# Two transformer blocks on one core: attention heads prepared in slices, key halves copied by DMA, chunk heads split out of PSUM, late consumers of powers, 128-row gates, offset half-width weights

## The chip, the cores and the metric

The kernel runs on one core of a Trainium2 chip. The metric is the time of one execution on the device, in microseconds (us). A core has five engines with a queue of instructions each: TensorE (PE, matrix products; the load of the stationary operand is shown apart as PEld), VectorE (DVE), ScalarE (ACT), GpSimd (POOL) and SyncE (SP, which here only issues DMAs). Each engine works through its queue in order and waits on semaphores for what other engines or DMAs must have finished. Products are summed in PSUM, everything else lies in SBUF.

## The reference

512 tokens of width 1024 pass through two blocks, in f32.

```python
# block 1 (first_block)
proj = rmsnorm(h) @ w_in            # q, k, v: 8 heads of 64; u, g of the gated branch; 8 forget gates
c = cumsum(log_sigmoid(gates))      # per head, along the tokens
p = softmax(causal(q k^T / 8 + c[query] - c[key]));  att = p v
uv = gelu(u, g);  sg = u * (w_spatial (128x128, lower triangle) @ rmsnorm(g) + b_spatial)
h = h + concat(att, sg) @ w_out
h = h + (silu(g) * a) @ w_down      # a, g: halves of the causal 3-tap convolution of rmsnorm(h) @ w_up
x = rmsnorm(h, norm_final_g)
# block 2 (second_block), with modulation from silu(c) @ w_ada
proj = modulated(rmsnorm(x)) @ w_in # latents of q (256) and kv (128), a rope key (32), ca: 8 chunk heads of 64
mla:  q = rope(rmsnorm(rmsnorm(q_lat) @ w_q_up)); k, v from kv_lat; mask by chunks of 64 tokens
ca:   q, k = rmsnorm(ca_q) g_q, rmsnorm(ca_k) g_k; softmax(q k^T / 8 + rel_bias)
x = x + g_a * (concat(mla, ca) @ w_out);  x = x + g_m * conv_ffn(modulated(rmsnorm(x)))
```

## The kernel before

Every product is made from halves: an operand is split into a high part (rounded to the fp32r format of TensorE) and a low part (the rest), and three matmuls hi·hi, hi·lo, lo·hi are summed. The names end in h and l (xnh, xnl; whi, wlo).

Weights stream from DRAM. `make_plan` (L276) lists all pieces in order of use, at most 128x1024 each. For each piece `load_split` (L335) issues a load on SP's queue into `wraw` (3 buffers), ACT casts it to `whi`, and DVE (for a few pieces POOL) subtracts to get `wlo`. A piece is requested when the product two pieces ahead of it takes its own. A plan entry ends with an offset: some pieces are written 192 elements into their buffers (`SKEW`). Before, only token-major pieces carry it, in which the weights are the moving operand.

The program has five stages: mix of block 1 (0 to 241.6 us of the span), FFN of block 1 (to 588), start of block 2 (to 664), attention of block 2 (to 882.6), FFN of block 2.

Attention is cut in strips: one head times 128 queries; 32 strips in block 1, 64 in block 2 (32 of chunk heads, then 32 of latent heads). A strip is: scores on PE (`strip_scores`, s<-kh,qs and s<-kl,qs); DVE adds the bias and takes the row minimum of the negated scores (L590, s and st); ACT takes the exponential (L594, p); one strip later PE transposes p (L603, s<-ident,p), DVE or ACT copies it out of PSUM (L605, pt); one strip after that PE multiplies it with the values (o<-vv,pt or o<-vc,pt). After eight strips a pair of heads is divided by its sums (L687, att), transposed (L695) and split into `mix`.

Between the strips of `attention` (L612) two lists of jobs advance (class `Fill`): `fill` holds products for PE, which cover the chain from scores to p; `bg` holds norms for DVE, ACT and POOL. `fill.upto(name)` runs all fill work up to a named product at once. PE's order is the order in which the program is written. The other engines are ordered by a list scheduler; `high_priority(offset)` moves work forward (AHEAD, 40) or back (BEHIND, 60) in it. Once set, each engine keeps its order.

A head is prepared `ahead` strips before its first scores, 2 in block 1, 4 in block 2. In block 1 that is a PE product which spreads one row of cumulated gates over 128 rows (mm<-cum,pick, 64 rows of contraction), the copies ch and cm, and `stack` (L659). That stacks the high and the low half of q on 128 partitions (qs) and the key parts kh and kl twice, so that two matmuls do the work of three: ACT copies kh twice, DVE subtracts kl twice, 64x512 each (L668, L669). In block 2 a pair of chunk heads is transposed into PSUM (L1596), copied to qf and kf (L1599, L1601), and stacked from there.

Reciprocal square roots of the norms are powers on POOL (L523). Three products use them on DVE: uv by ss (L1104, gated branch), ca by ssc (L1423, chunk heads), mqk by nw (L1514, latent heads). `final` (L912, x<-x,cols,mm, 16 operations on 128x256) is the last norm of block 1, and runs in the bg list of block 2.

PSUM has eight banks: four for products (mm), three for scores (s), one for values (o) during attention.

Of the kernel before, what the change touches and what calls it, by code (L numbers as in the profile page):

```python
# [229 lines left out]
BEHIND = 60  # L230
HALVES = (slice(0, 256), slice(256, 512))


class Kernel:
# [41 lines left out]
    def make_plan(self):  # L276
        i, plan = self.i, []

        def fm(name, tiles, kt0=0, nk=KT, pool=False, last=None):
            for n in tiles:  # L280
                for p in self.fm_pieces(i[name], n, kt0, nk):
                    plan.append((p, pool, None, 0))
            if last:
                plan[-1] = plan[-1][:2] + (last, 0)
# [8 lines left out]
        def parts(name, dest):  # L293
            for p in range(4):
                for g in range(2):
                    plan.append((i[name][p, g], False, dest.get((p, g)), 0))
# [35 lines left out]
        self.ada_left, self.pools, self.before = [], {}, []  # L332
# [191 lines left out]

    def rstd(self, ms, scale, bias):
# [52 lines left out]
    def strip_scores(self, hd, qi):  # L578
# [10 lines left out]
        for j, (cs, b) in enumerate(parts):  # L589
            nc.vector.tensor_tensor_reduce(  # L590
                out=s[:, cs], in0=s[:, cs], in1=b, scale=1.0, scalar=3e38 if j == 0 else st[:, j - 1:j],
                op0=ALU.add, op1=ALU.min, accum_out=st[:, j:j + 1])
# [19 lines left out]
    def attention(self, heads, fill, rate, bg, bgrate, mix, ahead=2, depth=1):  # L612
# [46 lines left out]
    def stack(self, pool, q, k, odd):  # L659


        nc = self.nc
        a, b = (slice(64, 128), slice(0, 64)) if odd else (slice(0, 64), slice(64, 128))
        qs, kh, kl = (pool.tile([P, 512], F32R, tag="st", name=nm) for nm in ("qs", "kh", "kl"))
        nc.scalar.copy(qs[a], q[a])
        nc.vector.tensor_tensor(out=qs[b], in0=q[a], in1=qs[a].bitcast(F32), op=ALU.subtract)
        for o in (a, b):
            nc.scalar.copy(kh[o], k[a])  # L668
            nc.vector.tensor_tensor(out=kl[o], in0=k[a], in1=kh[a].bitcast(F32), op=ALU.subtract)  # L669
        return [(qs, kh), (qs, kl)]  # L670
# [332 lines left out]
    def block1_mix(self, xn, x, evac, evac_last, norm_a):  # L1003
# [27 lines left out]
        cum = one.tile([64, 512], F32R, name="cum")  # L1031
        pick = one.tile([64, 8], F32R, name="pick")
        nc.vector.tensor_tensor(out=pick, in0=self.ident[0:64, 0:8], in1=self.ident[0:64, 32:40], op=ALU.add)
# [53 lines left out]
        def gate(j):  # L1087
# [57 lines left out]
        def qk(pr):  # L1145
            def ev(n, ps, cs):
                with self.tc.high_priority(offset=AHEAD):
# [4 lines left out]
                    else:  # L1152
                        kf[pr] = two.tile([P, 512], F32, tag="kf", name="kf")
                        nc.vector.tensor_tensor(out=kf[pr], in0=ps, in1=rrow, op=ALU.mult)
# [51 lines left out]
        def cumulate():  # L1206
# [5 lines left out]
            with self.tc.high_priority(offset=AHEAD):  # L1212
                nc.scalar.copy(cum, cp)
# [21 lines left out]
        def head(h):  # L1235
            def f(_):
                fill.upto(f"qk{h // 2}") if h > 1 else None
                with self.tc.high_priority(offset=AHEAD):
                    return prepare(h)

            def prepare(h):
                pr, odd = divmod(h, 2)
                sums, sh = self.sums(pairs, h)
                qs = self.stack(stk, qf[pr], kf[pr], odd)

                cp = self.bank()
                self.mm(cp, pick[:, h:h + 1].to_broadcast([64, P]), cum, True, True)
                ch = two.tile([P, 512], F32, tag="ch", name="ch")
                cm = two.tile([P, 512], F32, tag="cm", name="cm")
                nc.any.tensor_copy(out=ch, in_=cp)  # L1250
                nc.gpsimd.tensor_tensor(
                    out=cm.rearrange("p (b k) -> p b k", k=P),
                    in0=ch.rearrange("p (b k) -> p b k", k=P),
                    in1=cmask.unsqueeze(1).to_broadcast([P, 4, P]), op=ALU.add)

                def bias(qi):
                    d = slice(qi * P, (qi + 1) * P)
                    r = [(d, cm[:, d])]
                    if qi:
                        r.append((slice(0, qi * P), ch[:, 0:qi * P]))  # L1260
                    return r

                return dict(qk=qs, bias=bias, v=lambda kb: vv[:, kb, h * 64:(h + 1) * 64], sums=sh,
                            end=(sums, pr, mx, "mix"))
            return f

        cumulate()
        for _ in range(4):
# [3 lines left out]
                       lambda t: 1300, mix, ahead=2)  # L1272
# [56 lines left out]
    def block2_mix(self, xn, norm_b, final, evac, evac_last, norm_a):  # L1329
        nc, i = self.nc, self.i  # L1330
        ctx = ExitStack()
# [5 lines left out]
        stk = self.pool("stk2", 8, ctx=ctx)  # L1337
# [69 lines left out]
        def ca_norm(z, j):  # L1407
# [13 lines left out]
            for t in range(4):  # L1421
                v3 = ca_slice(t, z, j).rearrange("p (g d) -> p g d", d=64)
                nc.vector.tensor_tensor(out=v3, in0=v3, op=ALU.mult,  # L1423
# [271 lines left out]
```

## Time and profile before

| | us |
|---|---|
| median of 3 runs | 1242.46 (1242.16 to 1245.07) |
| profiled execution, its own time | 1242.75 |
| its span in the profile | 1240.9 |
| PE busy in the span | 1206.9 (97%) |
| mean granted clock of TensorE, share of full | 0.989 |

The profile's span is 1.85 us shorter than the execution's own time. In the rows below a start is in us from the span's start; the square brackets behind a timeline row give the idle time of the engine just before it and what ended it. PE's matmuls are pipelined: the next one starts before the last has ended, so what one costs is read from the distance of starts.

### The profile page before, as it was taken

What the parts mean: (1) busy time and instruction counts of PE and PEld (TensorE: products, weight loads), DVE (VectorE), ACT (ScalarE), POOL (GpSimd) and SP (SyncE); (2) the same over time, 40 slices, a digit from 0 to 9 for tenths busy, and PEclk for the clock granted to TensorE, in tenths of its full rate; (3) what the DMA queues carried; (4) which work ended last, traced back from release to release, by engine and by line L of the source; (5) the groups of instructions that cost most, each with busy time, mean ns of one, the idle gap of its engine ahead of it and who ended that gap; (6) DMA issues with size and microseconds to landing.
All of it is one profiled execution on the core that took longest, in us unless ns stands there. A gap on an engine that the chain in (4) does not pass through costs nothing.

```text
span 1240.9 us, 17330 instructions
## 1 busy us (share of the span) xinstructions
PE 1206.9 (97%) x6730; PEld 1049.5 (85%) x6730; DVE 792.5 (64%) x1415; ACT 539.2 (43%) x963; POOL 194.2 (16%) x208
## 2 busy tenths in 40 slices
PE   9999999999999999999998998899999999999998
PEld 6887878988888888888998897789988888888887
DVE  6555877688888886433666779766676566553221
ACT  6444544444444443223435555664554444442110
POOL 1457400300000000000344452501200000000000
PEclk9999999999999999999999999999999999999999
DMA  7321212156666656433122111110132222233330
GB/s 242 99 86 48 73 68 69 52 190 200 189 202 195 193 185 193 129 94 114 56 103 64 56 69 61 51 35 18 69 119 87 101 102 92 96 94 103 117 110 17
DMA packets 40033, 131.57 MB, mean 106 GB/s; under 512 B 4608, under 2 KB 5504, under 8 KB 39952
## 3 DMA queue, kind: packets, MB, share of 16 engines
q1 hardware_dynamic: 31536, 102.64, 25.2%
q10 hardware_dynamic: 8208, 27.27, 7.1%
q8 instruction: 52, 0.85, 0.3%
q0 software_dynamic: 208, 0.57, 0.2%
q14 instruction: 29, 0.24, 0.1%
HBM read 128.37 MB, written 2.10 MB: 105 GB/s over the span
## 4 chain that ended last, share of the span: by engine, by line
PE 85%; DVE 7%; POOL 4%; ACT 2%; issue 2%; DMA 1%; SPq 0%; POOLq 0%; ACTq 0%; DVEq 0%
PE mm L369 74%; PE s L369 4%; PE o L369 3%; PE s L603 2%; DVE wlo L348 1%; DVE nt L550 1%; DMA x<-in_xT_dram 1%; DVE ca L1423 1%; DVE s L590 0%; POOL ss L523 0%; POOL nw L523 0%; PE s L695 0%; DVE kl L669 0%; DMA cs<-in_c_dram 0%; PE mm L1635 0%
## 5 line engine op out<-in xcount | busy, mean ns | idle before, releaser
L348 DVE TENSOR_TENSOR wlo<-wraw,whi 128x1024 fp32r<-128x1024 f32 (+4 forms) x182 | 210.4, 1158 | 182.0 <-ACT whi L347 181.2
L347 ACT CAST whi<-wraw 128x1024 fp32r<-128x1024 f32 (+4 forms) x194 | 192.2, 994 | 281.3 <-PE mm L369 261.8
L369 PE MATMUL mm<-xnh,whi 128*128 128x512 f32 (+1 forms) x832 | 312.4, 375 | 1.1 <-DVE nt L550 0.6
L369 PE MATMUL mm<-xnl,whi 128*128 128x512 f32 (+1 forms) x832 | 311.0, 374 | 0.0
L369 PE MATMUL mm<-xnh,wlo 128*128 128x512 f32 (+1 forms) x832 | 310.7, 373 | 0.0
L369 PEld LDWEIGHTS mm<-xnh,whi 128*128 128x128 f32 x832 | 157.0, 189 | 28.7 <-PE mm L369 0.8
L369 PEld LDWEIGHTS mm<-xnh,wlo 128*128 128x128 f32 x832 | 157.1, 189 | 27.7
L369 PEld LDWEIGHTS mm<-xnl,whi 128*128 128x128 f32 x832 | 157.2, 189 | 27.1
L369 PE MATMUL mm<-gh,whi 128*128 128x512 f32 (+1 forms) x384 | 141.6, 369 | 1.1 <-DVE x L937 0.6
L369 PE MATMUL mm<-gl,whi 128*128 128x512 f32 (+1 forms) x384 | 141.3, 368 | 0.0
L369 PE MATMUL mm<-gh,wlo 128*128 128x512 f32 (+1 forms) x384 | 141.3, 368 | 0.0
L729 DVE SCALAR_TENSOR_TENSOR cv<-mm,cols,cv 128x510 f32<-128x510 f32 (+1 forms) x176 | 130.4, 746 | 2.6 <-ACT cv L727 0.6
L369 PE MATMUL mm<-whi,xnh 128*128 128x256 f32 (+3 forms) x304 | 97.7, 321 | 0.2 <-ACT xnh L812 0.2
L369 PE MATMUL mm<-wlo,xnh 128*128 128x256 f32 (+3 forms) x304 | 94.3, 310 | 0.2 <-DVE wlo L348 0.2
L369 PE MATMUL mm<-whi,xnl 128*128 128x256 f32 (+3 forms) x304 | 94.2, 310 | 0.1
L369 PEld LDWEIGHTS mm<-gh,whi 128*128 128x128 f32 x384 | 72.4, 188 | 13.6 <-DVE x L937 0.8
L369 PEld LDWEIGHTS mm<-gl,whi 128*128 128x128 f32 x384 | 72.4, 188 | 12.1
L369 PEld LDWEIGHTS mm<-gh,wlo 128*128 128x128 f32 x384 | 72.4, 188 | 12.0
L594 ACT ACTIVATE p<-s,st 128x128 f32<-128x128 f32 (+1 forms) x96 | 50.7, 528 | 69.7 <-DVE st L590 66.7
L998 DVE CUSTOM_DVE_ANT_0 wada<-wada,cs,cols 128x1024 f32<-128x1024 f32 x48 | 61.5, 1282 | 26.9 <-DMA wada<-in_w_ada_dram 26.7
L369 PE MATMUL mm<-mix,whi 128*128 128x256 f32 (+1 forms) x288 | 74.4, 346 | 2.7 <-ACT vm L1563 1.2
L727 ACT ACTIVATE cv<-mm,cols 128x512 f32<-128x512 f32 x88 | 67.6, 772 | 0.2 <-PE mm L369 0.2
(293 smaller groups left out, 1839.1 us busy)
## 6 DMA issues: line engine op xcount, KB each, us to landing
wraw<-in_w_up_dram SPq DMA_DIRECT2D x88, 512.0 KB, 3.4
wada<-in_w_ada_dram ACTq DMA_DIRECT2D x48, 512.0 KB, 3.6
wraw<-in_w_down_dram SPq DMA_DIRECT2D x32, 512.0 KB, 3.5
wraw<-in_w_out_dram SPq DMA_DIRECT2D x16, 512.0 KB, 3.4
wraw<-in_w_down_dram SPq DMA_DIRECT2D x16, 384.0 KB, 3.1
wraw<-in_w_qk_dram SPq DMA_DIRECT2D x8, 512.0 KB, 3.7
wraw<-in_w_v_dram SPq DMA_DIRECT2D x8, 256.0 KB, 4.9
x<-in_xT_dram SPq DMA_DIRECT2D x8, 256.0 KB, 6.4
```

What stands on the lines that cost most here:

```text
L347: nc.scalar.copy(hi[:, :n], raw[:, :n])
L348: (nc.gpsimd if pool else nc.vector).tensor_tensor(out=lo[:, :n], in0=raw[:, :n], in1=hi[:, :n].bitcast(F32), op=ALU.subtract)
L369: self.nc.tensor.matmul(out, lhsT, rhs, start=start, stop=stop, **kw)
L550: self.applied = nc.vector.scalar_tensor_tensor(out=t, in0=x[k][:, cs], scalar=gain(k), in1=r, op0=ALU.mult, op1=ALU.mult).ins
L594: nc.scalar.activation(out=p[:, :nk], in_=s[:, :nk], func=AF.Exp, bias=st[:, len(parts) - 1:len(parts)], scale=-1.0, accum_out=hd["sums"](qi))
L603: self.nc.tensor.transpose(s[:, c], p[:, c], self.ident)
L727: nc.scalar.activation(out=t, in_=ps, func=AF.Identity, scale=w[2], bias=self.col(cb, n))
L729: nc.vector.scalar_tensor_tensor(out=t[:, d:], in0=ps[:, :512 - d], scalar=w[2 - d], in1=t[:, d:], op0=ALU.mult, op1=ALU.add)
L998: nc.vector.tensor_tensor_reduce(out=w, in0=w, in1=self.cs, scale=1.0, scalar=self.col("b_ada_2", n), op0=ALU.mult, op1=ALU.add, accum_out ...
L1423: nc.vector.tensor_tensor(out=v3, in0=v3, op=ALU.mult, in1=ss[:, j, z, t].unsqueeze(2).to_broadcast([P, 4, 64]))
```

## The change

There are seven edits.

1. Consumers of powers: `late` makes the three DVE products by ss, ssc and nw issue after `self.urgent`, the row minimum of the strip written last (or the copy kf of block 1's keys).
2. Head preparation becomes a generator per head, whose slices (gates, q, k in block 1; q, k in block 2) are run one a strip from LEAD = 5 strips ahead. `fill.upto` for a head's product moves with the first slice.
3. The chunk heads of block 2 are stacked straight from PSUM: ACT and DVE read the transposes there, for both heads of the pair; qf and kf are gone, and the bank is held until all four operations of its pair are done.
4. The second half of kh and of kl is copied by a DMA from the first (64x512 f32, 128 KB, on SP's queue): 32 DMAs in place of 16 ACT and 16 DVE operations.
5. `cum` and `pick` get 128 rows (the new rows are zero), for 8 matmuls.
6. The offset of 192 elements is given to more weights, those whose products are 256 columns wide and in which the weights are the stationary operand: tiles 0, 1, NF, NF+1 of both w_up (2 x 192 matmuls), the last of both w_down (2 x 132), w_lat (144), and parts 2 and 3 of the first w_out (144): 936 matmuls.
7. `final` is queued in the first bg list of block 2's attention, and no longer behind the second half of the latent heads. The pool of stacked heads there has 12 buffers for 8.

```diff
+LEAD = 5
@@ make_plan
-        def fm(name, tiles, kt0=0, nk=KT, pool=False, last=None):
+        def fm(name, tiles, kt0=0, nk=KT, pool=False, last=None, skewed=()):
             for n in tiles:
                 for p in self.fm_pieces(i[name], n, kt0, nk):
-                    plan.append((p, pool, None, 0))
+                    plan.append((p, pool, None, SKEW // 4 if n in skewed else 0))
...
-                fm(up, [j, j + NF])
-            fm(down, range(KT), 0, NF, last=last)
+                fm(up, [j, j + NF], skewed=(0, 1, NF, NF + 1))
+            fm(down, range(KT), 0, NF, last=last, skewed=(KT - 1,))
...
-        parts("w_out", {(3, 1): ("mx", "mix", "mix")})
+        parts("w_out", {(3, 1): ("mx", "mix", "mix")}, (2, 3))
...
-        fm("w_lat", range(3))
+        fm("w_lat", range(3), skewed=range(3))
+    def late(self):
+        return self.tc.issue_after(self.urgent) if self.urgent else nullcontext()
@@ strip_scores
-            nc.vector.tensor_tensor_reduce(
+            self.urgent = nc.vector.tensor_tensor_reduce(
...
@@ attention
-        hd[0] = heads[0](0)
+        with self.tc.high_priority(offset=AHEAD):
+            slices(0)
         fill.run(rate(-1))
         for t in range(n + depth + 3):
-            for h, _ in seq[:t + ahead + 1]:
-                if h not in hd:
-                    hd[h] = heads[h](h)
             r = rate(t)
             if t < n:
                 h, qi = seq[t]
+                slices(h)
                 sc[t] = self.strip_scores(hd[h], qi)
+                for h in range(len(heads)):
+                    if 0 < seq.index((h, 0)) - t <= LEAD:
+                        slices(h, 1)
...
+    def stack_k(self, tiles, k, odd, scale=None):
+        nc, (_, kh, kl) = self.nc, tiles
+        a, b = HALF_P[::-1] if odd else HALF_P
+        if scale is None:
+            nc.scalar.copy(kh[a], k[a])
+            nc.vector.tensor_tensor(out=kl[a], in0=k[a], in1=kh[a].bitcast(F32), op=ALU.subtract)
+        else:
+            nc.scalar.activation(out=kh[a], in_=k[a], func=AF.Copy, scale=scale[a])
+            nc.vector.scalar_tensor_tensor(out=kl[a], in0=k[a], scalar=scale[a], in1=kh[a].bitcast(F32),
+                                           op0=ALU.mult, op1=ALU.subtract)
+        for t in (kh, kl):
+            nc.sync.dma_start(out=t[b].bitcast(F32), in_=t[a].bitcast(F32))
@@ spatial, and alike for ca by ssc and mqk by nw
-                nc.vector.tensor_tensor(out=v3, in0=v3, op=ALU.mult,
-                                        in1=ss[:, j, t].unsqueeze(2).to_broadcast([P, 4, 64]))
+                with self.late():
+                    nc.vector.tensor_tensor(out=v3, in0=v3, op=ALU.mult,
+                                            in1=ss[:, j, t].unsqueeze(2).to_broadcast([P, 4, 64]))
@@ block 1: gates, and a head in slices
-        cum = one.tile([64, 512], F32R, name="cum")
-        pick = one.tile([64, 8], F32R, name="pick")
+        cum = one.tile([P, 512], F32R, name="cum")
+        pick = one.tile([P, 8], F32R, name="pick")
...
+            fill.upto(f"qk{h // 2}") if h > 1 else None
...
+            self.mm(cp, pick[:, h:h + 1].to_broadcast([P, P]), cum, True, True)
...
+            yield
+            tiles = self.stacked(stk)
+            self.stack_q(tiles, qf[pr], odd)
+            yield
+            self.stack_k(tiles, kf[pr], odd)
+            yield
@@ block 2: chunk heads
+                for z, nm in ((0, "q"), (1, "k")):
+                    ps = self.bank()
+                    o = z * 512 + pr * P
+                    for t in range(4):
+                        nc.tensor.transpose(ps[:, t * P:(t + 1) * P], ca[t][:, o:o + P], self.ident)
+                    for y in range(2):
+                        if z == 0:
+                            self.stack_q(stacks[h + y], ps, y)
+                        else:
+                            self.stack_k(stacks[h + y], ps, y, gca)
+                    yield
...
```

Three places show how the instructions move.

DVE in block 1 around strip 8 (uv, ss: the gated branch and its powers; s, st: a strip's row minimum; kl, qs: a head's stack; ch: gates). Before:

```order
L666 TENSOR_TENSOR qs<-qf,qs 64x512
L669 TENSOR_TENSOR kl<-kf,kh 64x512 x2
L1098 TENSOR_SCALAR ss<-ss 128x16
L685 RECIPROCAL sums<-sums 128x8
L1104 TENSOR_TENSOR uv<-uv,ss 128x256 x3
L590 ISA s,st<-s,cm 128x128
L590 ISA st 128x1
L1104 TENSOR_TENSOR uv<-uv,ss 128x256
L590 ISA s,st<-s,cm 128x128
L590 ISA st 128x1
```

After:

```order
L687 TENSOR_TENSOR qs<-qf,qs 64x512
L694 TENSOR_TENSOR kl<-kf,kh 64x512
L1129 TENSOR_SCALAR ss<-ss 128x16
L715 RECIPROCAL sums<-sums 128x8
L1276 COPY ch<-mm 128x512
L597 ISA s,st<-s,cm 128x128
L597 ISA st 128x1
L1136 TENSOR_TENSOR uv<-uv,ss 128x256
L597 ISA s,st<-s,cm 128x128
L597 ISA st 128x1
L597 ISA s,st<-s,ch,st 128x128
L597 ISA st 128x1
L1136 TENSOR_TENSOR uv<-uv,ss 128x256 x2
```

The row minima of strips 8 and 9 stood behind three products by ss and now stand ahead of two of them; of a head's two subtractions kl one is gone, and a copy ch has come in.

PE in block 1 from strip 26 on (mm<-mix: part 0 and 1 of w_out's product, fill work; s<-kh,qs: a strip's scores; s<-ident,p: the transposes of the strip before). Before:

```order
L369 MATMUL mm<-mix,whi 128x256 x2
L369 MATMUL mm<-mix,wlo 128x256
L369 MATMUL mm<-mix,whi 128x256 x2
L369 MATMUL mm<-mix,wlo 128x256
L695 MATMUL s<-ident,att 128x128 x4
L369 MATMUL o<-vv,pt 128x64
L369 MATMUL s<-kh,qs 128x256
L369 MATMUL s<-kl,qs 128x256
L603 MATMUL s<-ident,p 128x128
L369 MATMUL o<-vv,pt 128x64 x2
L369 MATMUL s<-kh,qs 128x384
L369 MATMUL s<-kl,qs 128x384
```

After:

```order
L610 MATMUL s<-ident,p 128x128 x4
L372 MATMUL o<-vv,pt 128x64 x3
L372 MATMUL s<-kh,qs 128x256
L372 MATMUL s<-kl,qs 128x256
L610 MATMUL s<-ident,p 128x128
L372 MATMUL o<-vv,pt 128x64 x4
L372 MATMUL s<-kh,qs 128x256
L372 MATMUL s<-kl,qs 128x256
L610 MATMUL s<-ident,p 128x128 x2
L725 MATMUL s<-ident,att 128x128 x4
L372 MATMUL o<-vv,pt 128x64
L372 MATMUL s<-kh,qs 128x256
```

Before, the first strip with no fill work behind its scores is the one that follows the att transposes (strip 27); after, the strips are bare three earlier, since the fill work ran ahead.

SP's queue at the end of block 1's mix (wraw: a weight's load; kh, kl: the copy of a key half). Before:

```order
L338 DMA wraw<-in_w_qk_dram 128x1024 x4
L338 DMA wraw<-in_w_g_dram 128x1024 x2
L338 DMA wraw<-in_w_u_dram 128x1024 x4
L338 DMA wraw<-in_w_qk_dram 128x1024 x4
L338 DMA wraw<-in_w_out_dram 128x1024 x8
L338 DMA wraw<-in_w_up_dram 128x1024 x44
L338 DMA wraw<-in_w_down_dram 128x1024 x2
```

After:

```order
L341 DMA wraw<-in_w_qk_dram 128x1024
L341 DMA wraw<-in_w_out_dram 128x1024 x4
L700 DMA kh<-kh 64x512
L341 DMA wraw<-in_w_out_dram 128x1024
L700 DMA kl<-kl 64x512
L341 DMA wraw<-in_w_out_dram 128x1024
L700 DMA kh<-kh 64x512
L341 DMA wraw<-in_w_out_dram 128x1024
L700 DMA kl<-kl 64x512
L341 DMA wraw<-in_w_out_dram 128x1024
L341 DMA wraw<-in_w_up_dram 128x1024
L700 DMA kh<-kh 64x512
L700 DMA kl<-kl 64x512
L341 DMA wraw<-in_w_up_dram 128x1024 x3
```

The copies of heads 4 to 7 of block 1 stand between the loads of w_out and of w_up, and a load at the queue's head that waits for its buffer holds them.

## Rows read from the trace of the kernel before

**Rows 1.** Part 1 of the page: busy time, share of the span, instructions of each engine.
```profile
PE 1206.9 (97%) x6730; PEld 1049.5 (85%) x6730; DVE 792.5 (64%) x1415; ACT 539.2 (43%) x963; POOL 194.2 (16%) x208
```
**Rows 2.** Block 2's attention: stretch, length, busy PE, PEld, DVE, ACT, POOL, clock, DMA.
```profile
664.00:882.60 218.60, 203.72 (x1524) 191.96 (x1523) 163.07 (x379) 124.07 (x306) 69.07 (x77) 0.97 0.15 52
```
**Rows 3.** PE's waits: line that waits, for whom, us in total, times, longest.
```profile
PE s L603 <- ACT p L594: 14.5, 9, 2.9
```
**Rows 4.** Windows: first and last of eight stretches at the lower clock.
```profile
64.70:68.20 3.50, 3.50 (x10) 2.77 (x10) 3.40 (x7) 1.59 (x3) 0.68 (x1) 0.51 0.14 55
...
750.80:754.20 3.40, 3.03 (x14) 2.74 (x13) 2.40 (x6) 2.73 (x8) 0.04 (x1) 0.50 0.44 154
```
**Rows 5.** PE's timeline at 64 us: start, duration, line, out<-in, idle before and its end.
```profile
64.22 0.50 PE L369 MATMUL mm<-cum,pick 64*128 64x512 f32 x1 [2.04 <-DVE cum L1214]
...
65.18 0.63 PE L369 MATMUL mm<-xnl,whi 128*128 128x512 f32 x1
65.61 0.63 PE L369 MATMUL mm<-xnh,wlo 128*128 128x512 f32 x1
```
**Rows 6.** Windows in FFN 1: PE at the full clock, products of 512 columns.
```profile
300.00:340.00 40.00, 40.00 (x179) 33.10 (x178) 32.84 (x46) 17.56 (x24) 0.00 (x0) 1.00 0.62 196
```
**Rows 7.** DVE's timeline ahead of 64 us and at strip 8.
```profile
59.82 0.76 DVE L1104 TENSOR_TENSOR uv<-uv,ss 128x256 f32<-128x256 f32 x2 [3.02 <-POOL ss L523]
...
113.06 1.62 DVE L1104 TENSOR_TENSOR uv<-uv,ss 128x256 f32<-128x256 f32 x3 [2.92 <-POOL ss L523]
```
**Rows 8.** PE's timeline: strip 8 of block 1, and four places of block 2.
```profile
115.57 0.33 PE L603 MATMUL s<-ident,p 128*128 128x128 f32 x1 [2.90 <-ACT p L594]
...
704.36 0.66 PE L695 MATMUL s<-ident,att 128*128 128x128 f32 x4 [1.53 <-DVE att L687]
...
725.83 0.55 PE L603 MATMUL s<-ident,p 128*128 128x128 f32 x3 [2.46 <-ACT p L594]
...
749.28 0.33 PE L603 MATMUL s<-ident,p 128*128 128x128 f32 x1 [2.89 <-ACT p L594]
...
780.59 0.55 PE L603 MATMUL s<-ident,p 128*128 128x128 f32 x3 [1.40 <-ACT p L594]
```
**Rows 9.** DVE's timeline at the same places of block 2.
```profile
702.61 1.09 DVE L1423 TENSOR_TENSOR ca<-ca,ssc 128x256 f32<-128x256 f32 x3 [3.01 <-POOL ssc L523]
...
723.52 0.96 DVE L1514 TENSOR_TENSOR mqk<-mqk,nw 128x768 f32<-128x768 f32 x1 [3.03 <-POOL nw L523]
...
745.91 2.46 DVE L669 TENSOR_TENSOR kl<-kf,kh 64x512 fp32r<-64x512 f32 x2
...
753.02 6.35 DVE L912 SCALAR_TENSOR_TENSOR x<-x,cols,mm 128x256 f32<-128x256 f32 x16 [0.23 <-PE mm L369]
```
**Rows 10.** PE's timeline: a gate product and the matmul behind it.
```profile
78.23 0.49 PE L369 MATMUL mm<-cum,pick 64*128 64x512 f32 x1
78.65 0.44 PE L369 MATMUL s<-kh,qs 128*128 128x384 f32 x1
```
**Rows 11.** The chain in order of time: w_ck0's products (offset, moving), then w_lat's (none).
```profile
610.06 6.04 PE mm L369 x52
616.10 8.63 PE s L369 x72
```
**Rows 12.** PE's timeline: part 0's start, and two waits in the bare strips 27 to 30.
```profile
175.57 0.50 PE L369 MATMUL mm<-mix,whi 128*128 128x512 f32 x1 [0.79 <-DVE mix L715]
...
204.01 0.44 PE L603 MATMUL s<-ident,p 128*128 128x128 f32 x2 [0.95 <-ACT p L594]
...
207.12 0.66 PE L603 MATMUL s<-ident,p 128*128 128x128 f32 x4 [0.76 <-ACT p L594]
```
**Rows 13.** DMA issues: out<-in, count, KB each, median us to landing.
```profile
wraw<-in_w_kn_dram SPq DMA_DIRECT2D x2, 128.0 KB, 2.0
```
**Rows 14.** SP's queue, its waits in total.
```profile
SPq L338 <- DVE wlo L348: 869.9, 157, 31.3
```
**Rows 15.** DVE's timeline: four products beside a subtraction on POOL.
```profile
656.21 5.80 DVE L1423 TENSOR_TENSOR ca<-ca,ssc 128x256 f32<-128x256 f32 x4 [3.02 <-POOL ssc L523]
```

More of the change, by code (lines that the diff above doesn't have):

```diff
@@ L1 @@
-from contextlib import ExitStack
+from contextlib import ExitStack, nullcontext
 from itertools import chain
@@ L610, in strip_values, with attention @@
             self.mm(o, pt[:, kb * P:(kb + 1) * P], hd["v"](kb), kb == 0, kb == qi)
-    def attention(self, heads, fill, rate, bg, bgrate, mix, ahead=2, depth=1):
+    def attention(self, heads, fill, rate, bg, bgrate, mix, depth=1):
         last = len(heads) - 2
@@ L620, in attention, with slices @@
         hd, sc, pt, later, o = {}, {}, {}, [], None
-        hd[0] = heads[0](0)
+        def slices(h, count=99):
+            for _ in range(count):
+                if h not in hd:
+                    try:
+                        next(heads[h])
+                    except StopIteration as e:
+                        hd[h] = e.value
+        with self.tc.high_priority(offset=AHEAD):
+            slices(0)
         fill.run(rate(-1))
         for t in range(n + depth + 3):
-            for h, _ in seq[:t + ahead + 1]:
-                if h not in hd:
-                    hd[h] = heads[h](h)
             r = rate(t)
@@ L1212, in cumulate @@
             with self.tc.high_priority(offset=AHEAD):
-                nc.scalar.copy(cum, cp)
+                nc.scalar.copy(cum[0:64], cp)
                 nc.vector.tensor_tensor(out=cum[32:64], in0=cp[32:64], in1=cum[32:64].bitcast(F32),
@@ L1235, in head @@
         def head(h):
[L1236 to L1264, printed above, removed]
@@ L1265, in head @@
-            return f
+            fill.upto(f"qk{h // 2}") if h > 1 else None
+            pr, odd = divmod(h, 2)
+            sums, sh = self.sums(pairs, h)
+            cp = self.bank()
+            self.mm(cp, pick[:, h:h + 1].to_broadcast([P, P]), cum, True, True)
+            ch = two.tile([P, 512], F32, tag="ch", name="ch")
+            cm = two.tile([P, 512], F32, tag="cm", name="cm")
+            nc.any.tensor_copy(out=ch, in_=cp)
+            nc.gpsimd.tensor_tensor(
+                out=cm.rearrange("p (b k) -> p b k", k=P),
+                in0=ch.rearrange("p (b k) -> p b k", k=P),
+                in1=cmask.unsqueeze(1).to_broadcast([P, 4, P]), op=ALU.add)
@@ L1458, in cq0 @@
             bg.add("rope", rope())
+            bg.add("final", final)
         bg = Fill()
@@ L1513, in q_norm @@
                 rq = r[:, 2 * a:2 * a + 2].unsqueeze(3)
[L1514 removed]
+                with self.late():
+                    nc.vector.tensor_tensor(out=v, in0=v, in1=rq.to_broadcast([P, 2, 4, QK]), op=ALU.mult)
                 rt = self.pp.tile([P, 4, 2, 4, 16], F32, tag="p", name="rt")
@@ new lines, in ca_head @@
+            pr, odd = divmod(h, 2)
+            if pr >= 2:
+                fill.upto("ck1")
+                bg.upto("w_ck1")
+            elif pr == 0:
+                bg.upto("w_cq0")
+            sums, sh = self.sums(pairs, h)
+            bs = two.tile([P, 512], F32, tag="bs", name="bs")
+            nc.scalar.dma_start(out=bs, in_=i["relb"][h])
+            if not odd:
+                for z in range(2):
+                    stacks[h + z] = self.stacked(stk)
+                for z, nm in ((0, "q"), (1, "k")):
[9 more added lines that the diff above has]
+                    yield
@@ new lines, in ca_head, with bias, v @@
+            nc.vector.tensor_scalar(out=bs, in0=bs, scalar1=-1.0, scalar2=None, op0=ALU.mult)
+            nc.gpsimd.memset(bs[0:64, 448:512], BIG)
+            def bias(qi):
+                n = (qi + 1) * P
+                return [(slice(0, n), bs[:, 512 - n:512])]
+            def v(kb):
+                if pr >= 2:
+                    fill.upto("cv1")
+                return vc[:, kb, h * 64:(h + 1) * 64]
+            qs, kh, kl = stacks.pop(h)
+            return dict(qk=[(qs, kh), (qs, kl)], bias=bias, sums=sh, v=v,
+                        end=(sums, 4 + pr, one, mix_at[pr]))
@@ new lines, in mla_head, with bias @@
+        def mla_head(h):
+            pr, odd = divmod(h, 2)
+            c, hc = divmod(h, 4)
+            fill.upto(f"mla{c}")
+            bg.upto(f"mk{c}")
+            sums, sh = self.sums(pairs, 8 + h)
+            m = slice(0, QK)
+            parts = []
+            for src, scale in ((mq[c], None), (mk[c], gml[m])):
+                b = self.bank()
+                for t in range(4):
+                    nc.tensor.transpose(b[m, t * P:(t + 1) * P], src[t // 2][:, t % 2, hc], self.ident)
+                hi = stk.tile([P, 512], F32R, tag="st", name="hi")[m]
+                lo = stk.tile([P, 512], F32R, tag="st", name="lo")[m]
+                if scale is None:
+                    nc.scalar.copy(hi, b[m])
+                    nc.vector.tensor_tensor(out=lo, in0=b[m], in1=hi.bitcast(F32), op=ALU.subtract)
+                else:
+                    nc.scalar.activation(out=hi, in_=b[m], func=AF.Copy, scale=scale)
+                    nc.vector.scalar_tensor_tensor(out=lo, in0=b[m], scalar=scale,
+                                                   in1=hi.bitcast(F32), op0=ALU.mult, op1=ALU.subtract)
+                parts.append((hi, lo))
+                yield
+            (qh, ql), (kh, kl) = parts
+            def bias(qi):
+                n = (qi + 1) * P
+                return [(slice(0, n), mlam[:, 512 - n:512])]
+            return dict(qk=[(qh, kh), (qh, kl), (ql, kh)], bias=bias, sums=sh,
+                        v=lambda kb: vm[c][:, kb, hc * 64:(hc + 1) * 64],
+                        end=(sums, pr, one, f"ca{pr}"))
```

119 lines of the change are left out of this document (30 added, 89 removed).

## The prediction

> **What bounds the kernel now.** I read part 1 of the page first, then the windows by stage, PE's waits, the windows of PE's clock, and the timelines of PE and DVE at each gap. PE is busy 1206.9 of 1240.9 us [rows 1], so 34.0 us of idle time and the pace of PE itself are all that can be won. The reader should see that the idle time lies in the attention stages: block 2's attention alone leaves 218.6 − 203.72 = 14.9 us [rows 2]. There PE waits mostly for a strip's exponential, 14.5 us in nine waits [rows 3], that is, for DVE's row minimum ahead of it.
>
> A gap costs twice. The granted clock is at full in FFN 1, where 512 columns take 40.00/178 = 0.225 us [rows 6]. It is at half (1.2 of 2.4 GHz) in eight stretches of 3.4 to 3.5 us, of which the first and the last are shown [rows 4]. The first begins right after a 2.04-us gap, and its 512 columns take 65.61 − 65.18 = 0.43 us [rows 5]; so 3.5 us do 3.5 × 0.225/0.43 = 1.83 us of work, and 1.6 us are lost. In the last, where PE is busy 3.03 of 3.40 us, 3.03 × 0.48 = 1.4 us. I price a low-clock stretch at 1.6, the last one at 1.4.
>
> **The change part by part.** The sum is made against the profiled execution: 1242.75 us, which is its span plus 1.85 us and 0.3 us above the median of 1242.46.
>
> *Late consumers of powers.* DVE is in order, and five times it stands at a product whose power on POOL is not done. At 59.8 us it has waited 3.02 us for ss, and behind it stand kf, a weight's subtraction and cum [rows 7], for which PE waits 2.04 us [rows 5]. In the new order these two uv products stand behind the minima of strips 0 to 2, so gap and stretch go: 2.0 + 1.6 = 3.6 us. At strip 8 DVE waits 2.92 us and then does three products ahead of the minimum [rows 7]; PE waits 2.90 us [rows 8]. The new order has strip 8's minimum first: 2.9 + 1.6 = 4.5. At 702.6 the wait of 3.01 us stands ahead of att [rows 9], for which PE waits 1.53 us [rows 8]: 1.5 + 1.6 = 3.1. At 723.5 it is nw, 3.03 us [rows 9], and PE's gap is 2.46 us [rows 8]. In the new order this first product of nw still stands directly ahead of the next strip's minimum; only its beginning moves. Bounds: 0 (nothing moves) and 2.5 + 1.6 = 4.1; I take 2.0, since the operations that feed nw start earlier but the wait stays. At 780.6 the second product of nw is spread behind two minima, and the gap of 1.40 us [rows 8] goes: 1.4, with no stretch behind it. Sum: 3.6 + 4.5 + 3.1 + 2.0 + 1.4 = 14.6. What is late next at these places is the exponential itself, which follows the minimum at once.
>
> *Slices and direct split.* At 745.9 two subtractions kl of 1.23 us each stand ahead of a strip's minimum [rows 9], and PE's gap is 2.89 us [rows 8], the last low stretch behind it [rows 4]. Now one of the two is a DMA, the copy to qf is gone, and q and k come in different strips. The one subtraction alone gives 1.2; I take the whole 2.9 + 1.4 = 4.3, because what is left stands behind other minima.
>
> *Key halves by DMA.* 16 operations each leave ACT and DVE. Where neither is waited for that is worth nothing, and the place at 745.9 is counted. A load of 128 KB lands 2.0 us after its issue [rows 13]. No row shows one from SBUF to SBUF; between 0 and twice that I take 2.0. Where a head is prepared strips ahead it is covered: a strip of block 2 takes 218.6/64 = 3.4 us [rows 2]. The first heads of block 2 have no such lead: 2.0 in place of the 1.23 us of the removed subtraction, so +0.8 (0 to 2.0).
>
> *128-row gates.* A gate product holds PE from 78.23 to 78.65, 0.42 us [rows 10]; 128 rows of contraction take 0.225 [rows 6]. Eight of them: 8 × 0.195 = 1.6 at most and 0 at least. I take 1.2, because a first matmul behind a switch of operands is a little longer than one in a row.
>
> *Offset half-width weights.* Of neighbours at full clock, those with the offset take 6.04/52 = 116.2 ns, those without 8.63/72 = 119.9 ns [rows 11]. There the offset is on the moving operand; here it is put on the stationary one, which no row shows. Bounds: half of 225 ns is 112.4, so 936 × 7.5 ns = 7.0 us won, and as a loss the same difference of 3.7 ns, 936 × 3.7 = 3.5 us. I take the neighbouring row as a gain, 3.5.
>
> The Trainium skill ("TensorE: Matmul & The Clock Gate", Step-by-step: what each phase is for) says that the load of weights and the moving operand come through separate interfaces to SBUF. By that rule the offset would do nothing, and the sum would lack its 3.5 us; the difference of the two rows speaks against it, and no run here yet shows the stationary side.
>
> *What the moves cost.* A head's fill work is now asked for at LEAD = 5 strips, so `fill` runs three to four strips ahead in block 1, and three more strips at the end are bare, as the order of PE shows. Two waits of 0.95 and 0.76 us fall on the four bare strips before [rows 12]: 1.71/4 × 3 = 1.3, and one more low stretch, 1.6. Upper bound: three waits like the 2.90 us of [rows 8]. Part 0 of w_out now begins right behind work that feeds it, with a wait like the 0.79 us before [rows 12]: 0.8. `final`, 6.35 us on DVE in 16 pieces of 0.40 [rows 9], goes from a place after the last chunk heads to strips 3 to 6 of block 2; a piece ahead of a minimum delays it by 0.40, and fill work covers most: 1.0 (0 to 6.4). The bank of a pair's transposes is held for the second head's operations, 1.23 us each [rows 9], eight times: 0 to 9.8. I take 1.0, since PE seldom turns to the fourth bank between strips.
>
> *Sum.* Gains 14.6 + 4.3 + 1.2 + 3.5 = 23.6; costs 0.8 + 1.3 + 1.6 + 0.8 + 1.0 + 1.0 = 6.5. Net −17.1: 1242.75 − 17.1 = 1225.7 us.
>
> **The rivals.**
>
> *1. The late products meet POOL.* Four ca products beside POOL's subtraction took 5.80 us [rows 15], where three alone took 1.09 [rows 9], so 1.45 for four: 4.3 us more. If the late products at strip 8, 702 and 723 meet POOL's next operation in this way, the next minimum is late by as much, and their 4.5 + 3.1 + 2.0 = 9.6 are lost: 1235.3. For it speaks that POOL multiplies uv right after the first product; against it, that the two other minima now stand ahead.
>
> The Trainium skill ("SBUF — State Buffer", SBUF: two separate sides) says that a DVE operation with two SBUF inputs and a GpSimd operation that reads SBUF exclude each other for the whole operation. The 5.80 us agree with that in kind.
>
> *2. The key halves come late (slower).* The copies stand in SP's queue between weight loads, and a load waits there for its buffer, on average 869.9/157 = 5.5 us, at most 31.3 [rows 14]. With 2.0 us to land that is 7.5, against a lead of about three strips, 10 us. Seven places have such a load ahead of them: heads 4 to 7 of block 1 and the second to fourth pair of block 2. If each comes 3 us late, with a stretch of 1.6 behind it, that is 7 × 4.6 = 32.2 and 1257.9 us. It decides from 17.1/7 = 2.4 us a place, stretch included. Against it: the wait's average is less than the lead, and in block 2 loads are few in these strips.
>
> *3. The burst starves the strips.* At strip 11 of block 1 the product of heads 4 and 5 runs at once, and the gated branch's DVE and POOL work comes in front of strip 12's minimum. If there, at part 0's start and at part 1's end PE waits 2.9 + 1.6 us, 13.5 are given back: 1239.2, no measurable change. PE's burst is work it must do anyhow; the wait behind it is what would count.
>
> *4. The change of pace doesn't come.* Neither offset nor 128 rows change PE's pace: 1225.7 + 3.5 + 1.2 = 1230.4. This lies in the range of the forecast and needs no chance of its own.
>
> **How the numbers follow.** The forecast with its own bounds (1218 to 1234; rival 4 within) gets 0.54, rival 1 0.16, rival 3 0.12, rival 2 0.13; 0.05 stays for better than 1218, where all unknown terms go well: gains 3.6 + 4.5 + 3.1 + 4.1 + 1.4 + 4.3 + 1.6 + 7.0 = 29.6 and no costs, 1213.1. The range is 1213 to 1245: it holds all but rival 2 and some tails. A measurement of this kernel can tell about 0.3% from no change, 3.7 us. Faster (below 1238.7): 0.54 + 0.16 + 0.05 = 0.75. Same: rival 3, 0.12. Slower (above 1246.2): rival 2, 0.13.
>
> **What would show it.** PE's waits for the exponential should fall from 14.5 us to about 7, and the eight low stretches to four or five, with none at 64, 116, 706 and 751 us. The gate product should hold PE for about 0.27 us, and w_lat's 72 matmuls 8.4 us for 8.63. The span of bare strips at the end of block 1's attention should grow from four to seven, with waits for the exponential there. I am wrong if PE waits for kh or kl at a strip's scores (rival 2), if a uv, ca or mqk product takes several times its former duration ahead of a minimum (rival 1), or if new waits stand at strips 11 to 16 of block 1 (rival 3).

## The result and the profile after

The changed kernel takes 1226.8 us in the median (1225.62 to 1227.99, 4 runs), the kernel before 1243.76 in the same runs: a ratio of 0.986, 95% interval 0.984 to 0.988. The forecast was 1225.7. The profiled execution of the changed kernel took 1225.62 us, with a span of 1223.9. So the total came out as forecast; the terms did not all.

The page's first part (columns as in [rows 1]), PE's longest waits (as in [rows 3]) and the windows of the two stretches at the lower clock (as in [rows 4]) of the changed kernel:

```profile
PE 1193.0 (97%) x6730; PEld 1038.9 (85%) x6730; DVE 780.2 (64%) x1392; ACT 526.5 (43%) x946; POOL 190.5 (16%) x209
```

```profile
PE mm L372 <- DVE x L877: 4.7, 3, 2.7
PE s L610 <- ACT p L601: 3.6, 6, 1.3
PE mm L1633 <- DVE ca L1457: 3.4, 2, 2.2
PE mm L1633 <- DVE qs L687: 3.0, 2, 2.7
PE mm L372 <- DVE mix L745: 2.8, 2, 2.6
PE mm L372 <- DVE kf L1186: 2.3, 1, 2.3
```

```profile
601.20:604.70 3.50, 3.28 (x16) 2.98 (x16) 1.56 (x7) 0.77 (x2) 2.96 (x5) 0.51 0.07 28
659.30:662.70 3.40, 3.40 (x19) 3.40 (x18) 2.34 (x4) 1.80 (x4) 0.00 (x0) 0.50 0.11 33
```

PE's busy time falls by 13.9 us with the same 6730 matmuls, so that part is pace: six low stretches at 1.6 us, the offset and the gates (1.9 and 1.3 below) make 12.8 of it. Its idle time falls by only 3.1 us, from 34.0 to 30.9, because new waits come where old ones went. Of eight low stretches two are left, both at the start of block 2; all six in the attention stages are gone. The wait for the exponential falls from 14.5 us to 3.6. Four waits are new or longer, each between 2.3 and 2.7 us; PE's timeline of the changed kernel has them here:

```profile
128.28 0.50 PE L372 MATMUL mm<-xnh,whi 128*128 128x512 f32 x1 [2.29 <-DVE kf L1186]
...
148.86 0.70 PE L372 MATMUL mm<-uv,wsp 128*128 128x256 f32 x2 [2.59 <-DVE mix L745]
...
230.35 0.39 PE L372 MATMUL mm<-xnh,whi 128*128 128x256 f32 x1 [2.72 <-DVE x L877]
...
708.79 0.63 PE L1633 MATMUL mm<-ident,ca 128*128 128x128 f32 x4 [2.66 <-DVE qs L687]
```

Before, 230.35 has a counterpart of 0.46 us and 708.79 one of 0.33; the other two had none. The one at 148.86 stands in the second half of the gated branch's products, directly ahead of part 0 of w_out. The 0.79 us that [rows 12] puts at part 0's start belongs to part 1: before, part 0 starts at 157.69 without a wait, and part 1 at 174.28. None of the four has a low stretch behind it in this execution.

Where the time goes is best seen by when the same strip's scores begin in both profiles (after minus before, us): strip 0 −4.0, strip 8 −4.6, strip 10 −9.8, early in FFN 1 −2.9, late in FFN 1 −3.3, strip 32 −3.3, strip 42 −1.4, strip 43 −4.1, strip 49 −6.0, strip 55 −12.8, strip 66 −15.6, end −17.0. Block 1's attention wins 9.8 us by strip 10 and gives back 6.9; block 2's wins 12.3.

### The profile page after: what moved, and what is told of

Its sections match the earlier page's. It is cut to its first block, busy times and chain, and to the rows that moved or that the text cites. A ratio compares the mean times of both kernels' runs of the same rounds, so it can differ in the third digit from the quotient of the medians.

```text
span 1223.9 us, 17406 instructions
## 1 busy us (share of the span) xinstructions
PE 1193.0 (97%) x6730; PEld 1038.9 (85%) x6730; DVE 780.2 (64%) x1392; ACT 526.5 (43%) x946; POOL 190.5 (16%) x209
## 4 chain that ended last, share of the span: by engine, by line
PE 84%; DVE 6%; POOL 4%; issue 2%; ACT 2%; DMA 1%; SPq 0%; ACTq 0%; DVEq 0%; POOLq 0%
PE mm L372 74%; PE s L372 4%; PE o L372 3%; PE s L610 2%; POOL wlo L351 1%; ACT whi L350 1%; DVE wlo L351 1%; DVE s L597 1%; DVE ca L1457 1%; DMA x<-in_xT_dram 1%; POOL gelu L1111 0%; PE mm L1667 0%; DVE nt L557 0%; ACT p L601 0%; PE s L725 0%
```

## The experiments

Eleven of the twelve change one thing, e10 and e11 against e7 and the others against the kernel that their name gives; e12 joins three. All times are medians; the ratio is to the kernel before in the same runs, with its 95% interval.

| run | us | ratio |
|---|---|---|
| e1 changed, products not late | 1244.25 | 1.001 (0.9994 to 1.0027) |
| e2 changed, no offset | 1229.72 | 0.989 (0.987 to 0.991) |
| e3 changed, final back | 1239.32 | 0.997 (0.995 to 0.998) |
| e4 changed, key halves by engines | 1232.91 | 0.992 (0.989 to 0.994) |
| e5 before, late products alone | 1235.71 | 0.992 (0.989 to 0.995) |
| e6 changed, gates of 64 rows | 1228.14 | 0.986 (0.983 to 0.989) |
| e7 changed, lead 3 in block 1 | 1219.38 | 0.979 (0.976 to 0.983) |
| e8 changed, FFN 1's banks | 1224.39 | 0.984 (0.980 to 0.987) |
| e9 before, final alone | 1247.3 | 1.003 (1.002 to 1.005) |
| e10 e7, k slice later | 1220.21 | 0.980 (0.977 to 0.982) |
| e11 e7, w_ck1 by DVE | 1217.77 | 0.979 (0.977 to 0.980) |
| e12 e7, e11 and q first | 1222.78 | 0.982 (0.980 to 0.985) |

**e1 and e5: the late products.**

```diff
     def late(self):
-        return self.tc.issue_after(self.urgent) if self.urgent else nullcontext()
+        return nullcontext()
```

> The changed kernel (1226.8) with the three late products issued where the scheduler wants them; all else as changed. Theory 1 (a product that waits for a power ahead of a row minimum stops PE): gaps of about 2.0, 2.9, 1.5 and 1.4 us come back near 62, 110, 700 and 775 us, 7.8 us in all, and with up to three stretches at the lower clock (1.6 each) 1234 to 1240. Rival (the waits only move, the slices did the work): within 2 us of 1226.8.

e5 adds `late` and its three uses to the kernel before, and nothing else.

> The kernel before with the late products alone. Theory 1: it takes the gaps at 62, 113, 703 and 780 us (2.0, 2.9, 1.5, 1.4) and the stretches behind three of them (1.6 each), 12.6 us: 1230, and the low-clock stretches fall from eight to five. Rival (the gain comes from several edits together, the waits alone move): 3 to 5 us, 1238 to 1240.

e1 loses the whole gain, 17.4 us, and ends past the theory's upper bound of 1240: without the late products the other six edits are worth nothing measurable. Its waits stand where the theory put them, and the one at strip 8 is longer than before. The timelines of DVE, POOL and PE in e1:

```profile
109.65 5.72 DVE L1136 TENSOR_TENSOR uv<-uv,ss 128x256 f32<-128x256 f32 x4 [2.36 <-POOL ss L526]
115.30 0.29 DVE L597 CUSTOM_DVE_ANT_0 s<-s,cm 128x128 f32<-128x128 f32 x1
```

```profile
109.58 2.39 POOL L351 TENSOR_TENSOR wlo<-wraw,whi 128x1024 fp32r<-128x1024 f32 x1
```

```profile
116.25 0.33 PE L610 MATMUL s<-ident,p 128*128 128x128 f32 x1 [4.26 <-ACT p L601]
```

All four products now stand ahead of strip 8's minimum, and PE waits 4.26 us, where it was 2.90 [rows 8]. They take 5.72 us, where three took 1.62 [rows 7], beside a weight's subtraction on POOL: the mechanism of rival 1, here on the path. There are eight low stretches again.

e5 alone wins 9.2 us, less than the 12.6 expected. PE's timeline of e5 shows why: two new waits come near 117 us and one at 702 (for DVE's copy of mqk, which is no power), and the gap that was at 780 stays, 1.40 us at 770.87. The gap at 745 us before, which is not due to a power, stays as expected, at 739.15.

```profile
116.76 0.63 PE L698 MATMUL s<-ident,att 128*128 128x128 f32 x4 [1.08 <-DVE att L690]
...
118.55 0.51 PE L369 MATMUL s<-kh,qs 128*128 128x512 f32 x1 [0.98 <-ACT pt L608]
...
702.22 0.69 PE L1603 MATMUL mm<-ident,ca 128*128 128x128 f32 x4 [1.97 <-DVE mqk L1497]
...
739.15 0.33 PE L606 MATMUL s<-ident,p 128*128 128x128 f32 x1 [2.86 <-ACT p L597]
...
770.87 0.55 PE L606 MATMUL s<-ident,p 128*128 128x128 f32 x3 [1.40 <-ACT p L597]
```

So the late products are worth 9.2 us alone, the other edits −0.3 alone, and both together 17.0. About half of the gain belongs to the combination. No run undoes the slices or the direct split by themselves; what those two are worth is argued below from the place, and not shown.

**e2: the offset.** The offset of the plan's entries becomes 0 for the weights of edit 6:

```diff
-                    plan.append((p, pool, None, SKEW // 4 if n in skewed else 0))
+                    plan.append((p, pool, None, 0))
...
-                    plan.append((i[name][p, g], False, dest.get((p, g)), SKEW // 4 if p in skewed else 0))
+                    plan.append((i[name][p, g], False, dest.get((p, g)), 0))
```

The lines show the size too: `SKEW` is 192 and a piece gets `SKEW // 4`, so the offset is 48 elements of 4 bytes, 192 bytes in all, and not 192 elements as the description of the change has it. The last piece of the first w_down (36 matmuls) goes into another buffer without offset, so the edit reaches 900 matmuls, not 936.

> The changed kernel without the offset on the 936 matmuls' weights. The prediction's term: 3.5 us slower, 1230.3. Rival (the two profiles' own milestones: w_lat's stretch differs by 0.05 us, up and down products by 0.2 to 0.6 each): 1.4 us slower, 1228.2, and w_lat's 72 matmuls take 119.9 ns in both.

The median is 2.9 us slower; the two profiles, both at a mean clock of 0.997, differ by 1.9 us of span (1225.8 against 1223.9). The chain in order of time has w_lat's 72 matmuls, first of the changed kernel, then of e2:

```profile
612.98 8.48 PE s L372 x72
```

```profile
612.91 8.64 PE s L372 x72
```

That is 117.8 ns against 120.0. Over all half-width matmuls of either FFN, counting intervals at full clock, it is 117.7 to 118.1 ns with the offset and 119.8 to 119.9 without. 2.1 ns × 900 = 1.9 us, the difference of the spans: between prediction and rival, and on the stationary side too. The Trainium skill's rule of separate interfaces ("TensorE: Matmul & The Clock Gate", Step-by-step: what each phase is for), read as the prediction read it, would have made it 0; the measurement decides.

**e3 and e9: final.** e3 queues `final` behind the second half of the latent heads, as before; e9 moves it forward in the kernel before, alone.

```diff
             bg.add("rope", rope())
-            bg.add("final", final)
...
                 bg.add("kr", kr_rope())
+            else:
+                bg.add("final", final)
```

> The changed kernel with the 16 operations of final queued again behind the second half of the latent heads. Theory (the prediction's term, final costs about 1.0 to 1.4 us among the early strips and nothing was won where it left): 1 us faster, 1225.8, strips 36 to 38 start 1.4 us earlier. Rival (final was part of the crowd on DVE at 745 to 760 us): 2 to 6 us slower, with waits for the exponential near 735 to 750.

> The kernel before with final alone moved to the first bg list of block 2's attention. Prediction's term: about 1 us slower, 1245. Theory from e3 (on DVE, which is in order, the 16 pieces of final, 6.35 us in one run, stand ahead of a strip's minimum and crowd out the operations of the next strips): 3 to 8 us faster, 1236 to 1241, with the gaps at 749 and 755 us shorter. Rival (final only matters when heads are prepared five strips ahead): within 2 us of 1244.

The sign depends on what stands beside it. Moved alone it costs 2.9 us, more than the term of 1.0, and the theory of 3 to 8 us faster fails; taken back out of the changed kernel it costs 12.5, past both expectations. In e3 DVE's timeline has it in one run, and PE's has a wait some strips later:

```profile
746.24 6.35 DVE L942 SCALAR_TENSOR_TENSOR x<-x,cols,mm 128x256 f32<-128x256 f32 x16
```

```profile
777.39 0.90 PE L610 MATMUL s<-ident,p 128*128 128x128 f32 x3 [3.75 <-ACT p L601]
```

In the 30 us from 735 DVE is busy 27.25 us in e3 and 25.58 in the changed kernel. What stands there is the preparation of the latent heads, now five strips ahead, and `final` delays the norms that it needs: the last step ahead of their power (nw on DVE) starts at 766.75 us, 9.8 us later than in the changed kernel, where the strips around it are about 6 us late. A product by nw and two subtractions of weights then stand ahead of strip 63's minimum, which ends at 775.1, and its exponential waits on until 776.56 for POOL, which works on mqk. That is where the 3.75 us are; ACT's timeline of e3:

```profile
776.56 0.69 ACT L601 ACTIVATE p<-s,st 128x512 f32<-128x512 f32 x1 [3.58 <-POOL mqk L1359]
```

From strip 42 to 66 e3 falls 9.1 us behind the changed kernel, and 3.3 more at the end of the attention, with low stretches at 711, 776 (10.2 us long) and 871 us. The wait at that end, 2.52 us for ACT's sq, stands in e10 as well, which leaves `final` alone, so those 3.3 us can't be put down to `final`'s own work. A fourth stretch, at 230 us, is no part of it: that gap is 2.7 us in both kernels, and only e3 shows a stretch there, which costs it 2.7 us. In e9 nothing is prepared earlier, and the pieces mainly add to the early strips: 3.2 us between strips 32 and 43, among them a wait of PE for att of 2.37 us where it was 1.53 [rows 8].

**e4: the key halves.** ACT and DVE make both halves again, in place of the two DMAs.

```diff
+        for o in (a, b):
...
-        for t in (kh, kl):
-            nc.sync.dma_start(out=t[b].bitcast(F32), in_=t[a].bitcast(F32))
```

> The changed kernel with both halves of kh and kl made by ACT and DVE again (16 operations of 0.62 and 16 of 0.69 to 0.77 us come back, 32 DMAs go). Theory: neither engine is waited for at most of these places, 0 to 2 us slower, 1226.8 to 1228.8. Rival (the subtraction that went was what PE waited for at 745 us): 3 to 5 us slower with a gap of about 2 us near 708 or 736. If the DMAs themselves held something up it would be faster.

6.1 us slower, past both; between executions of the two kernels at the same mean clock it is 5.1 us (at 0.997) and 4.5 to 5.5 (at 0.994). It is no single gap: PE's waits for the exponential are 5.2 us for 3.6, for att 2.6 for 0.8, spread over both attention stages, and at 865 us one of 1.73 for x is new. The DMAs hold nothing up: PE waits for one once, 0.2 us, though they take twice the time of the small weight loads [rows 13]. The DMA issues of the changed kernel:

```profile
kh<-kh SPq DMA_DIRECT2D x16, 128.0 KB, 4.2
kl<-kl SPq DMA_DIRECT2D x16, 128.0 KB, 3.6
```

**e6: the gates.** `cum` and `pick` have 64 rows again.

> The changed kernel with gates of 64 rows again. The prediction's term: 8 products, 0.15 us each, 1.2 us slower, 1228.0; the next matmul starts 0.42 us behind a gate product again. Rival: the place, not the rows, sets what such a product costs: 0.

1.3 us slower by the medians, within the intervals. The rows settle it. PE's timeline, of the changed kernel and of e6:

```profile
67.42 0.40 PE L372 MATMUL mm<-cum,pick 128*128 128x512 f32 x1
67.65 0.28 PE L372 MATMUL mm<-whi,xnh 128*128 128x256 f32 x1
```

```profile
67.73 0.49 PE L372 MATMUL mm<-cum,pick 64*128 64x512 f32 x1
68.15 0.39 PE L372 MATMUL mm<-whi,xnh 128*128 128x256 f32 x1
```

0.23 us from start to start against 0.42, at the same place: the rows, not the place. Seven of the eight show it, 1.3 us; the eighth, between two products of the gated branch, keeps 0.42 in both, so the place counts there.

**e7: the lead in block 1.**

```diff
-                    if 0 < seq.index((h, 0)) - t <= LEAD:
+                    if 0 < seq.index((h, 0)) - t <= lead:
```

with `lead=3` for block 1 and 5 for block 2.

> The changed kernel with heads of block 1 prepared from 3 strips ahead (for 5). Theory (the early request for the products of heads 4 to 7 made the new waits at 128, 149 and 189 us and the bare strips): those waits, 2.3 + 2.6 + 1.5, shrink by half or more, 3 to 5 us faster, 1222 to 1224. Rival (the heads come late): PE waits at a head's first scores, as long or longer than now, 1227 to 1231.

7.4 us faster, more than expected and the best single step. PE's waits in e7, for p, kf, mix and x as in the changed kernel's list above:

```profile
PE s L610 <- ACT p L601: 2.7, 4, 0.9
PE mm L372 <- DVE kf L1186: 1.5, 1, 1.5
...
PE mm L372 <- DVE mix L745: 1.0, 2, 0.8
...
PE mm L372 <- DVE x L877: 0.5, 1, 0.5
```

Against 3.6, 2.3, 2.8 and 4.7 that is 7.7 us. So the lead of five strips in block 1 made these waits; the run moves the request for the products of heads 4 to 7 and the slices together and doesn't part them. Part of the last line is chance, as e8 shows.

**e8: FFN 1's banks.**

```diff
-            self.open_psum(c2, mm=6, r=2)
+            self.open_psum(c2, r=2, mm=6)
```

> The changed kernel; FFN 1 opens its PSUM pools in the other order, so that its second product no longer lies in the bank of the last product of the mix. Theory (the new wait of 2.72 us at 230 us is for that bank, which the scheduler happened to give to the last product): the wait falls to 0.5 us, 2.2 us faster, 1224.6. Rival (the wait is for the normalised input, which comes as late): no change.

The median falls by 2.4 us, which the two intervals alone don't tell from nothing; the waits show more. PE's wait for x in e8, 4.7 us in the changed kernel:

```profile
PE mm L372 <- DVE x L877: 2.0, 2, 1.4
```

The wait at 230 us is gone, though nothing but the order of the banks was changed, so it was for a bank: in the changed kernel the last product of the mix lay in the one that FFN 1's second product takes. Before, the same wait is 0.46 us, and e7's longest for x is 0.5. No edit meant that: the allocation follows the schedule.

**e10, e11, e12: what is left of block 2.** e10 puts one more strip between a pair's q and k slice. e11 takes POOL out of w_ck1's pieces (`pool=j > 1` for `pool=j > 0`). e12 joins e7, e11 and `high_priority(offset=AHEAD)` around the q halves of chunk heads.

> The kernel of e7 (1219.4), with the k slice of a pair of chunk heads one strip further behind its q slice. Theory (PE's 2.66-us wait at the second pair's k transposes is for the bank that DVE's two qs operations hold): the wait goes, 2.7 us faster, with up to one low stretch less 1215 to 1217. Rival (the wait moves to the next user of a bank, or the key halves now land late): 1219 to 1222.

> The kernel of e7 (1219.4), with the low parts of the two w_ck1 pieces made by DVE instead of POOL. Theory (four ca products take 5.9 us only because POOL reads SBUF at the same time): they take about 1.5 us, PE's two waits for ca at 647 and 649 us (1.2 + 2.25) nearly go, 3 to 5 us faster, 1214.5 to 1216.5. Rival (the products are slow for another reason, or DVE loses as much with the two subtractions): 5.9 us again, 1219 to 1221.

> The kernel of e7 (1219.4) with the low parts of w_ck1 by DVE (e11, 1217.8), and with the q halves of chunk heads 40 places further forward in the scheduler, so that the second of the pair's two qs operations stands ahead of krs, a row minimum and a weight's subtraction. Theory (PE waits at 700 us for the bank that these two operations hold): the second ends about 1.8 us earlier, the wait falls from 2.66 to 0.9 us, 1214.5 to 1216.5. Rival (strip 44's minimum, now later by 0.7 us, becomes the wait, or the bank's next user waits again): 1217 to 1219.

In e10 the wait only changes hands: the bank's next user is a product of the fill work, and waits the same 2.65 us (PE's timeline of e10):

```profile
702.33 0.36 PE L372 MATMUL mm<-whi,xnh 128*128 128x256 f32 x1 [2.65 <-DVE qs L687]
```

e11 shows the size of POOL's part. DVE's timeline, of e7 and of e11:

```profile
643.85 5.89 DVE L1457 TENSOR_TENSOR ca<-ca,ssc 128x256 f32<-128x256 f32 x4 [3.02 <-POOL ssc L526]
```

```profile
645.50 1.43 DVE L1457 TENSOR_TENSOR ca<-ca,ssc 128x256 f32<-128x256 f32 x4 [3.02 <-POOL ssc L526]
```

The same four products take 1.43 us when POOL subtracts nothing beside them. This is the exclusion that the Trainium skill states ("SBUF — State Buffer", SBUF: two separate sides). But PE wins little: its waits for ca go, and one of 2.88 us for kl comes at strip 32's scores, behind the two weights' subtractions and the stacking; 1217.8 is not told apart from e7. In e12 the wait at 700 us is halved and the other half comes back 2 us later at the next product, this time for ACT's mqk, much as the rival had it:

```profile
700.85 0.63 PE L1633 MATMUL mm<-ident,ca 128*128 128x128 f32 x4 [1.41 <-DVE qs L687]
...
702.85 0.58 PE L372 MATMUL mm<-whi,xnh 128*128 128x256 f32 x1 [1.37 <-ACT mqk L1526]
```

The median of 1222.8 is past both expectations. Its five runs split with the clock: 1217.2 at a mean of 0.997, 1222.2 to 1223.7 at 0.992 to 0.993. Why this version has more low stretches than e11 is open.

## Why the prediction was right, point by point

- **Late products, 14.6.** Right in mechanism and place at four of five: the steps in the starts are 4.0 by strip 0 (3.6), 5.3 at strip 8 to 10 (4.5), 2.7 at strip 43 (3.1), 1.9 by strip 49 (2.0). The fifth, 1.6 by strip 64 (1.4), came another way: e5 keeps that gap, and in the changed kernel the product by nw there (763.22 us) no longer waits for its power, presumably because the heads are prepared earlier. Undone the late products cost 17.4, done alone they give 9.2.

```profile
763.22 0.95 DVE L1550 TENSOR_TENSOR mqk<-mqk,nw 128x768 f32<-128x768 f32 x1
```

- **Slices and direct split, 4.3 at 745 us.** The step from strip 51 to 55 is 6.8. The part that I gave wholly to the slices is shared: of this step 1.1 us are lost in e3, with `final` back, and 0.9 in e4, without the DMAs. The rest is the slices' and the direct split's by its place alone; no run undoes those.
- **Key halves, no gain of their own and 0.8 of cost.** Wrong: e4 says 6.1. I looked for one place where the removed operations were waited for; they cost a little at many.
- **Gates, 1.2.** Right: 1.3 by the rows.
- **Offset, 3.5.** Mis-sized: 2.1 ns and 1.9 us for 3.7 ns and 3.5 us. The neighbouring row [rows 11] was of another operand, and a mixture: 24 of its 52 matmuls have the offset, 24 use a buffer without it, 4 are 128 columns wide. The second half of w_ck0 in the kernel before is clean, 24 with the offset and then 24 without, 114 and 118 ns each. So the size for the moving operand was right by luck, and it doesn't carry over to the stationary one.

```profile
624.58 0.29 PE L369 MATMUL mm<-whi,xnh 128*128 128x256 f32 x1
...
627.31 0.40 PE L369 MATMUL mm<-wsplit,xnh 128*128 128x256 f32 x2
...
630.14 0.29 PE L369 MATMUL mm<-whi,xnh 128*128 128x288 f32 x1
```

- **Block 1's costs, 0.8 + 1.3 + 1.6.** Places were named (part 0's start, bare strips) and priced too low: 6.9 us were given back between strip 10 and FFN 1. Rival 3's place, the burst at strip 11, was real (2.29 us). The 2.59 us stand just ahead of part 0, and the 0.79 that priced it was read at part 1. The low stretch that I added did not come, and the bare strips themselves cost little; the bank at 230 us (e8) was not foreseen.
- **final, 1.0.** The early strips' cost is there: 1.5 us between strips 35 and 38. What failed is that the prediction gave the place it left no value, without a reason; putting it back there costs the changed kernel 12.5 us.
- **Banks held, 1.0.** One place, 2.66 us, and 0.3 at another.
- **Low stretches.** I counted five fewer and one new; in the profiled execution it was six fewer and none new.

So the mechanism of the largest term was right, but that the total fits to 1 us is in part luck: it stands on errors of opposite sign. The gains of edits 4 and 7 were missed, and block 1's new waits and the offset were mis-sized the other way. The amounts of the runs can't be added up, since each edit's worth depends on the others. Rival 1's mechanism is in the trace, but in the changed kernel nobody waits for it: in DVE's timeline of the changed kernel one late product takes 2.60 us beside POOL, and strip 9's minimum behind it is still in time.

```profile
105.73 2.60 DVE L1136 TENSOR_TENSOR uv<-uv,ss 128x256 f32<-128x256 f32 x1 [2.10 <-POOL ss L526]
```

Rival 2 did not come about.

## What to carry to other kernels

On an engine that works in order, look for an instruction that waits for a slow engine and stands ahead of the one that the bound engine needs; order it behind, and do it together with whatever thins out the same engine: here the first alone gave about half and the rest alone nothing. A longer lead is not free: it pulls whole products forward, and their evacuation and norms land ahead of someone else's minimum; choose the lead by stage (5 to 3 in one stage gave 7.4 us here). A move's price is that of the place it leaves in the new schedule, not in the old.

## What the hardware showed that was not expected

- The same gap is followed by a low stretch in one program or execution and not in another: 2.72 us at 230.35 us had none in the changed kernel, 2.68 us had one in e1 and e3. Executions of the changed kernel took 1225.6 and 1225.8 us at a mean clock of 0.997, 1228.0 and 1227.8 at 0.994.
- A contraction over 64 rows holds PE longer than one over 128: 0.42 us against 0.23 for 512 columns.
- A copy of 128 KB from SBUF to SBUF landed 3.6 to 4.2 us after its issue, where a load of the same size takes 2.0 [rows 13].
